# A decoder block on one core: the gate of the GLA branch applied in the merge instead of in the chunk loop

## The chip, the core and the metric

The kernel runs on one core of one Trainium2 chip. A core has five engines with a queue of instructions each, which they take in order: TensorE (PE; its weight loads are listed apart as PEld), VectorE (DVE), ScalarE (ACT), GpSimd (POOL) and SyncE (SP). Here SP does nothing but issue the DMA transfers. The engines wait for each other by semaphores. The metric is the device time of one execution in microseconds, and the median of several runs stands for a kernel.

## The reference

One layer of a hybrid decoder block on 1024 tokens with 1024 channels, all in float32: a Mamba-2 branch (SSD) and a gated linear attention (GLA) side by side, a merge of the two, cross-attention to 256 memory tokens and a SwiGLU FFN. What the change touches is the end of the GLA branch and the merge:

```
def gla_mixer(q, k, v, r, a1, w_a2, b_a, norm_g):
    ...                                     # chunked scan: o of shape (token, head, 256)
    o = rmsnorm(o, norm_g).reshape(Bsz, S, GLA_DV)
    return (o * jax.nn.silu(r.astype(jnp.float32))).astype(q.dtype)

def hybrid_mixer(n, ...):
    ...
    merged = jax.nn.sigmoid(g_ssd) * (y_ssd @ w_up_ssd) + jax.nn.sigmoid(g_gla) * (y_gla @ w_up_gla)
    return merged @ w_o

h = h + hybrid_mixer(rmsnorm(h, norm_mix), ...)
```

The norm works on each head's 256 channels, so its weights are a vector of 256, and two columns of 128 serve all eight blocks of 128 channels. The gate r, the two gates g and the queries, keys and values all come out of one large product with `w_in`.

## The kernel before

Activations lie with channels on the partitions: eight blocks of 128 channels by 1024 tokens, or 512 tokens for a half. Every float32 operand of a large product is split into a high and a low part in TensorE's faster float32 format (`split`, line 223: a copy on ACT, a subtraction on DVE), and three products are added up. The products with `w_in` and with the FFN's weights are done by a Strassen-Winograd scheme of seven products (`Unit`), the merge's products directly (`dense`, line 1192).

The program is written as Python generators that `run` (line 439) interleaves: for each step of the main one, so many steps of the side ones as their rate says. What is written that way is a first order only. Each instruction has a priority by its place in the program, `ahead` and `prio` put some before others, and a planner orders each engine's instructions from modelled times. That order is then fixed: on the chip an engine whose next instruction is not ready stands still, even if a later one could go.

Stages that matter here, by their time in the profiled execution:

- SSD, to about 660 us. Beside it, products for r, q, k and the first gates run on TensorE; r goes ungated to `sr_d` in DRAM.
- GLA, about 660 to 832 us (`GLA`, line 999, and `gla_steps`, line 1082). Eight chunks of 128 tokens run beside the products for the gates `gs` and `gg`, with a priority 1000 places ahead. For each chunk `load` and `load_qk` fetch queries, keys, decays, r and values by SP. `decay` multiplies queries and keys by exponentials (Exp on ACT, the products on DVE). `attend` makes the scores and transposes the keys (their copy is `kt`). `out` computes the chunk's output, and its Squares with accumulation (line 1065), a root on DVE and POOL, and a scaled copy (line 1068) make the norm. `scan` updates the state. `norm` transposes the output on PE; DVE takes it out of PSUM, multiplies by the norm's weights and by Silu(r), and writes it into the buffer of the queries and keys, which is stored to `yg_d`. `gate` is the Silu, one ACT instruction of 128x1024. It stands at the end of a chunk for the next one, while r is loaded two chunks ahead. `qk`, `sr`, `bd` and `v` have two buffers each.
- The merge, from 846 us. Three products in a row, each eight output blocks by two halves of tokens, 24 matmuls of 512 columns apiece: `y_ssd @ w_up_ssd`, `y_gla @ w_up_gla`, and the merged one with `w_o`. Beside the first, `fetch` (line 1214) loads `yg_d` by blocks of channels into the operand buffers of the second, and splits them. The weights are split one output block ahead into a ring of two (`Left`, line 1146, the tile `wd`). After each output half `post_ys` or `post_yg` applies a Sigmoid on ACT and a multiplication on DVE (`gated`, line 1283). Half rows of other operands come through `quad` (line 1138), with six buffers, `ga`. `presum` (line 1236) prepares sums of the FFN's weights beside the three products: 55 steps, five for each 256 rows (a load of 1 MB, four sums and four stores of 256 KB).
- After that cross-attention, the FFN (1376 to 1980 us) and the last norm, which the change leaves as they are, but for the residual's sum (`residual`, line 1297).

```
        def load(s):
            ...
            s.sr = gl.tile([P, 8, CH], F32, name="sr", tag="sr", bufs=2)
            SP.dma_start(s.sr, sr_d[:, tk].rearrange("(k p) s -> p k s", p=P))
```

Of the kernel before, what the change touches and what calls it, by code (L numbers as in the profile page):

```python
# [9 lines left out]
F32 = mybir.dt.float32  # L10
F32R = mybir.dt.float32r
I32 = mybir.dt.int32
AF = mybir.ActivationFunctionType
ALU = mybir.AluOpType
AX = mybir.AxisListType

P = 128
TOK = 1024
D = 1024
NB = D // P  # L20
# [8 lines left out]
CH = 128  # L29
# [49 lines left out]
def block_kernel(ctx: ExitStack, tc: tile.TileContext, t: dict, out: bass.AP):  # L79
    nc = tc.nc  # L80
    now = [0.0]
    PE, ACT, SP = Tensor(nc.tensor, now), nc.scalar, nc.sync
    DVE, POOL = Meter(nc.vector, now, 0.06, 1.04e-3), Meter(nc.gpsimd, now, 0.08, 2.25e-3)
# [15 lines left out]
    def dram(name, *shape):  # L99
        return dr.tile(list(shape), F32, name=name, tag=name)  # L100

    xT_d = dram("xT_d", D, TOK)
    h1_d = dram("h1_d", D, TOK)
# [6 lines left out]
    sr_d = dram("sr_d", D, TOK)  # L110
    v_d = dram("v_d", TOK, D)
    gs_d = dram("gs_d", D, TOK)
    gg_d = dram("gg_d", D, TOK)
    ys_d = dram("ys_d", D, TOK)
    yg_d = dram("yg_d", D, TOK)
# [9 lines left out]
    def bank(dt=F32):  # L125
        return ps.tile([P, 512], dt, name="bank", tag="bank", bufs=4)

    add = lambda e, o, a, b: e.tensor_tensor(o, a, b, ALU.add)
    sub = lambda e, o, a, b: e.tensor_tensor(o, a, b, ALU.subtract)
    mul = lambda e, o, a, b: e.tensor_tensor(o, a, b, ALU.mult)  # L130
    ahead = lambda: tc.high_priority(offset=AHEAD)
    ALL = slice(0, HALF)
    half = lambda j: slice(j * HALF, (j + 1) * HALF)
# [60 lines left out]
    def col(name, i=0):  # L194
        which, at = gcol[name]
        return cols[:, which, at + i:at + i + 1]
# [26 lines left out]
    def split(src, hi, lo, e=None):  # L223
        ACT.activation(hi, src, AF.Copy)  # L224
        sub(e or DVE, lo, src, hi)
# [213 lines left out]
    def run(main, *rest, prio=0):  # L439

        owed = [0.0] * len(rest)
        for _ in main:
            for i, (g, rate) in enumerate(rest):
                owed[i] += rate
                while owed[i] >= 1.0:
                    owed[i] -= 1.0
                    with tc.high_priority(offset=prio):
                        next(g, None)
# [90 lines left out]
    for k in range(NB):  # L539
        p = bank()  # L540
# [298 lines left out]
    qk = w_in_units(Q0, 2, store_rows(q_d)) + w_in_units(K0, 2, store_rows(k_d))  # L839
# [25 lines left out]
    class SSD:  # L865
# [62 lines left out]
        def gate(s):  # L928
            s.y = sp_.tile([P, 4, CH], F32, name="y", tag="y", bufs=3)
            for k in range(4):  # L930
                DVE.scalar_tensor_tensor(s.y[:, k], s.L[:, k], dcol[:, s.g * 4 + k:s.g * 4 + k + 1],
                                         s.py[:, k * P:(k + 1) * P], ALU.mult, ALU.add)
            mul(POOL, s.y, s.y, s.L[:, 4:8])
            sq = sp_.tile([P, 4, CH], F32, name="sq", tag="sq", bufs=1)
            ACT.activation(sq, s.y, AF.Square)
            s.rd = sp_.tile([P, CH], F32, name="rd", tag="rd", bufs=2)
            DVE.tensor_reduce(s.rd, sq.rearrange("p k s -> p s k"), AX.X, ALU.add)
# [53 lines left out]
    gl = pool("gla", 1, stack=st4)  # L991
# [7 lines left out]
    class GLA:  # L999
# [3 lines left out]
            s.c, s.tk = c, slice(c * CH, (c + 1) * CH)  # L1003

        def load_qk(s):
            s.qk = gl.tile([P, 8, CH], F32, name="qk", tag="qk", bufs=2)
            for i, d in enumerate((q_d, k_d)):
                SP.dma_start(s.qk[:, 4 * i:4 * i + 4], d[:, s.tk].rearrange("(k p) s -> p k s", p=P))

        def load(s):  # L1010
            tk = s.tk
            s.bd = gl.tile([P, 4, CH], F32, name="bd", tag="bd", bufs=2)
            SP.dma_start(s.bd, bd_d[:, tk].rearrange("(k p) s -> p k s", p=P))
            s.sr = gl.tile([P, 8, CH], F32, name="sr", tag="sr", bufs=2)
            SP.dma_start(s.sr, sr_d[:, tk].rearrange("(k p) s -> p k s", p=P))
            s.v = gl.tile([P, D], F32, name="v", tag="v", bufs=2)
            SP.dma_start(s.v, v_d[tk, :])

        def gate(s):
            ACT.activation(s.sr, s.sr, AF.Silu)  # L1020

        def decay(s):
            e = gl.tile([P, 4, CH], F32, name="e", tag="e", bufs=1)
# [46 lines left out]
        def norm(s):  # L1070
            for a in range(2):
                p = bank()
                for b in range(4):
                    k = 2 * b + a
                    PE.transpose(p[:, b * P:(b + 1) * P], s.o[:, k // 2, (k % 2) * P:(k % 2) * P + P], ident)

                y, g = (x.rearrange("p (b a) s -> p a b s", a=2)[:, a] for x in (s.qk, s.sr))
                DVE.scalar_tensor_tensor(y, p.rearrange("p (b s) -> p b s", s=CH), col("gla_norm", a), g,
                                         ALU.mult, ALU.mult)
            SP.dma_start(yg_d[:, s.tk].rearrange("(k p) s -> p k s", p=P), s.qk)  # L1080

    def gla_steps():
        it = [GLA(c) for c in range(NCH)]
        it[0].load_qk()
        it[0].load()
        it[1].load_qk()
        it[1].load()
        yield
        it[0].decay()
        it[0].start()  # L1090
        yield
        it[0].attend()
        it[0].gate()
        yield
        for i, a in enumerate(it):
            b = it[i + 1] if i + 1 < len(it) else None
            c = it[i + 2] if i + 2 < len(it) else None
            a.out()
            yield
            if b and i:  # L1100
                b.load_qk()
            a.scan()
            yield
            if b:
                b.decay()
                b.start()
            yield
            a.norm()
            yield
            if b:  # L1110
                b.attend()
            if b:
                b.gate()
            if c:
                c.load()
            yield
# [11 lines left out]
    ysg_d = dram("ysg_d", D, TOK)  # L1128
# [9 lines left out]
    def quad(src, base, i, j):  # L1138
        q = rp.tile([P, HALF], F32, name="ga", tag="ga")
        SP.dma_start(q, src[base + i * P:base + (i + 1) * P, half(j)])  # L1140
        return q
# [41 lines left out]
    def hl(slots_, k):  # L1183
        if callable(slots_[k]):
            slots_[k] = slots_[k]()
        return slots_[k]
# [5 lines left out]
    def dense(no, ins, post, pre=lambda o, j: None, js=JS):  # L1192

        todo = [(o, j) for o in range(NB) for j in (js if o + 1 < NB else js[::-1])]
        got = [pre(*x) for x in todo[:2]]
        for n, (o, j) in enumerate(todo):
            w = left[NB * no + o]
            if n + 2 < len(todo):
                got.append(pre(*todo[n + 2]))
            cur = got[n]  # L1200
            p = acc()
            m = 0
            for k in range(NB):
                for a, b in ((0, 0), (0, 1), (1, 0)):
                    PE.matmul(p, w[:, a, k], ins[k][:, b, half(j)], start=m == 0, stop=m == 3 * NB - 1)
                    m += 1
            with ahead():
                post(o, j, p, cur)
            yield

    EVEN, ODD = ("op",) * 8, ("op",) * 6 + ("aux",) * 2
    i_ys, i_yg, i_wo, i_xq, i_q, i_xo = (paired(x) for x in (EVEN, ODD, EVEN, ODD, EVEN, EVEN))

    def fetch(src, dst):

        for k in range(NB):
            x = hl(dst, k)
            raw = x[:, 1].bitcast(F32)
            SP.dma_start(raw, src[k * P:(k + 1) * P, :])
            ACT.activation(x[:, 0], raw, AF.Copy)  # L1220
            sub(DVE, x[:, 1], raw, x[:, 0])
            yield

    get_ys = fetch(ys_d, i_ys)
    for n, _ in enumerate(group(gg[3:], B)):
        if n == 0:
# [7 lines left out]
    s1 = Stats(rp)  # L1234
# [25 lines left out]
    def quad_of(src):  # L1260
        return lambda o, j: quad(src, o * P, 0, j)
# [19 lines left out]
        return got_g[n][j]  # L1281

    def gated(g, p):
        ACT.activation(g, g, AF.Sigmoid)
        mul(DVE, g, p, g)

    def post_ys(o, j, p, g):
        gated(g, p)
# [5 lines left out]
        add(either(g), g, g, y)  # L1294
        into(i_wo, o, j, g)

    def residual(store, stats, gain, put):
        def post(o, j, p, q):
            add(DVE, q, p, q)
            SP.dma_start(store[o * P:(o + 1) * P, half(j)], q)  # L1300
            put(o, j, q, col(gain, o))
            stats.take(j, q)
        return post
# [7 lines left out]
    def waiting(g, n):  # L1311
        for _ in range(n):
            yield
        for _ in g:
            yield

    early = presum()
    run(dense(0, i_ys, post_ys, lambda o, j: gate(gs_d, o, j)), (fetch(yg_d, i_yg), 0.5), (waiting(early, 5), 1.0))
    run(dense(1, i_yg, post_yg, lambda o, j: (gate(gg_d, o, j), quad(ysg_d, o * P, 0, j))), (early, 1.0))
    run(dense(2, i_wo, residual(h1_d, s1, "norm_xattn", put_xq), quad_of(xT_d)), (early, 1.0))  # L1320


    kv = []
# [84 lines left out]
    for n in range(len(at) + 2):  # L1408
        a = at[n] if n < len(at) else None
        b = at[n - 1] if 0 < n <= len(at) else None  # L1410
# [17 lines left out]
    for u in range(D_FF // 256):  # L1428
# [5 lines left out]
        gate = Unit(t["w_ffn_in"], 0, 256 * u, post=gpost, key="aux")  # L1434
# [174 lines left out]
    for u in range(1, len(gu)):  # L1609
        gate, up = gu[u]  # L1610
# [8 lines left out]
    for x, (n, k, kn) in enumerate(todo):  # L1619
        name = CHAIN[n]  # L1620
# [58 lines left out]
```

## Time and profile before

| | us |
|---|---|
| median of three runs | 1998.22 |
| lowest and highest run | 1995.6, 1999.11 |
| profiled execution (first to last instruction) | 2000.0 |
| PE busy | 1933.5 |
| DVE busy | 1330.8 |
| ACT busy | 866.3 |
| POOL busy | 658.0 |
| GLA stage | 665 to 832 |
| first product of the merge | 846.4 to 933.4 |

The page gives no other time of the profiled execution than its span, which lies 1.8 us above the median. "Busy" is the time in which an engine has an instruction under way; matmuls are pipelined, so PE can be busy without being at its peak. An idle time of PE is put down to what released it. A line number can be that of a helper: line 73 is every DVE and POOL instruction, line 51 every matmul, line 55 every transpose. There the tile names tell which is meant: `whi` and `wlo` are a weight's split parts, `o` on a DVE row is an output of a `w_in` product, `o` on a row of lines 1065 and 1068 the GLA output.

### The profile page before, as it was taken

The page shows a single profiled execution, that of the slowest core. Times are in us where ns is not written, and L with a number is a line of the kernel's source. Part 1 is how long each engine was busy: PE and PEld are TensorE (multiplying, and loading weights), DVE is VectorE, ACT ScalarE, POOL GpSimd, SP SyncE. Part 2 cuts the span into 40 slices and gives each one's busy share as a digit, 9 for nine tenths or more (in the row PEclk, how much of TensorE's full clock was granted, in tenths as well). Part 3 has the DMA queues.
Part 4 walks back from the last instruction along what each step waited for, and adds up shares of the span by engine and source line. Part 5 has one row for each costly group of instructions (what it writes and reads, how often), then busy time and mean ns, then how long its engine had stood idle before and what let it go on. Part 6 is the DMA issues. An engine that isn't in the chain of part 4 may idle for free.

```text
span 2000.0 us, 26313 instructions
## 1 busy us (share of the span) xinstructions
PE 1933.5 (97%) x9772; PEld 1619.0 (81%) x9772; DVE 1330.8 (67%) x1869; ACT 866.3 (43%) x1486; POOL 658.0 (33%) x482
## 2 busy tenths in 40 slices
PE   6899999999999999999999999999999999999998
PEld 6799677787777877888888888877888888878887
DVE  5856579979887566643553427478777777784465
ACT  7434745455553555543223226453333333354243
POOL 3521253445654121112442100155444444430002
PEclk9899999999999999999999999999999999999999
DMA  9332233365663754697674310333224223176463
GB/s 303 137 123 76 97 127 116 107 199 162 181 192 103 213 162 158 226 394 242 252 249 163 106 43 22 126 124 124 79 90 134 93 85 119 72 269 220 153 228 126
DMA packets 242019, 309.59 MB, mean 155 GB/s; under 512 B 16586, under 2 KB 164276, under 8 KB 241892
## 3 DMA queue, kind: packets, MB, share of 16 engines
q1 hardware_dynamic: 241892, 307.92, 46.1%
q8 instruction: 77, 1.26, 0.3%
q14 instruction: 50, 0.41, 0.1%
HBM read 211.07 MB, written 96.80 MB: 154 GB/s over the span
## 4 chain that ended last, share of the span: by engine, by line
PE 69%; DVE 12%; DMA 7%; ACT 5%; issue 3%; POOL 3%; SPq 0%; POOLq 0%; DVEq 0%; ACTq 0%
PE acc L51 61%; PE bank L51 7%; DVE wlo L73 3%; DVE cv L73 2%; DVE o L73 1%; PE bank L55 1%; DMA raw<-in_w_in_dram 1%; DMA h_d<-ga 1%; DMA sr<-sr_d 1%; ACT whi L224 1%; DMA csb<-cs_d 1%; POOL sa L73 1%; DMA xt<-in_x_dram 1%; DMA fr<-act_d 1%; DVE fs L73 1%
## 5 line engine op out<-in xcount | busy, mean ns | idle before, releaser
L51 PE MATMUL acc<-hl,wd 128*128 128x512 f32 x1920 | 439.2, 390 | 0.2 <-DVE hl L73 0.2
L51 PEld LDWEIGHTS acc<-hl,wd 128*128 128x128 f32 x1920 | 360.0, 188 | 75.3 <-DVE hl L73 0.6
L73 DVE TENSOR_TENSOR wlo<-raw,whi 128x512 fp32r<-128x512 f32 x264 | 243.1, 925 | 64.9 <-ACT whi L224 64.5
L224 ACT ACTIVATE whi<-raw 128x512 fp32r<-128x512 f32 x272 | 169.7, 628 | 237.0 <-PE acc L51 208.1
L73 DVE TENSOR_TENSOR o<-acc,o 128x512 f32<-128x512 f32 (+1 forms) x256 | 172.5, 675 | 105.8 <-PE acc L51 91.1
L51 PE MATMUL acc<-fs 128*128 128x512 f32 (+1 forms) x792 | 156.0, 356 | 1.8 <-ACT o L1574 1.7
L51 PEld LDWEIGHTS acc<-fs 128*128 128x128 f32 x792 | 130.6, 189 | 22.8 <-ACT o L1574 2.1
L73 POOL TENSOR_TENSOR raw<-raw,sa 128x512 f32<-128x512 f32 x48 | 65.0, 1354 | 253.8 <-DVE wlo L73 250.8
L224 ACT ACTIVATE fs<-fr 128x1024 fp32r<-128x1024 f32 (+1 forms) x84 | 80.1, 984 | 112.9 <-PE acc L51 38.6
L73 DVE TENSOR_TENSOR fs<-fr,fs 128x1024 fp32r<-128x1024 f32 (+1 forms) x84 | 99.8, 1218 | 38.5 <-ACT fs L224 38.0
L224 ACT ACTIVATE whi<-sa 128x512 fp32r<-128x512 f32 x96 | 59.9, 627 | 107.5 <-PE acc L51 107.4
L73 POOL TENSOR_TENSOR sa<-raw 128x512 f32<-128x512 f32 x47 | 75.8, 1613 | 82.0 <-DMA raw<-in_w_in_dram 44.8
L73 DVE TENSOR_TENSOR wlo<-sa,whi 128x512 fp32r<-128x512 f32 x96 | 82.8, 863 | 19.0 <-ACT whi L224 17.6
L224 ACT ACTIVATE wd<-raw 128x1024 fp32r<-128x1024 f32 x40 | 42.2, 1058 | 104.9 <-PE acc L51 104.4
L73 DVE TENSOR_TENSOR wd<-raw,wd 128x1024 fp32r<-128x1024 f32 x40 | 53.9, 1349 | 50.5 <-ACT wd L224 50.0
L73 POOL TENSOR_TENSOR raw<-raw 128x512 f32<-128x512 f32 x48 | 83.0, 1730 | 5.0 <-DVE sa L73 5.0
L51 PE MATMUL acc<-B21h,whi 128*128 128x512 f32 x192 | 76.3, 398 | 3.1 <-ACT o L353 3.1
L51 PE MATMUL acc<-T1h,whi 128*128 128x512 f32 x192 | 76.3, 397 | 2.8 <-ACT whi L224 2.8
L51 PE MATMUL acc<-B22h,wlo 128*128 128x512 f32 x192 | 77.0, 401 | 1.2 <-DVE wlo L73 1.2
L51 PE MATMUL acc<-B22h,whi 128*128 128x512 f32 x192 | 75.2, 392 | 2.6 <-DVE o L73 1.5
L51 PE MATMUL acc<-T4h,whi 128*128 128x512 f32 x192 | 75.9, 395 | 1.5 <-DVE o L73 1.5
L51 PE MATMUL acc<-T1h,wlo 128*128 128x512 f32 x192 | 76.8, 400 | 0.5 <-DVE wlo L73 0.5
(386 smaller groups left out, 4771.6 us busy)
## 6 DMA issues: line engine op xcount, KB each, us to landing
raw<-in_w_in_dram SPq DMA_DIRECT2D x26, 1024.0 KB, 6.1
raw<-in_w_ffn_in_dram SPq DMA_DIRECT2D x22, 1024.0 KB, 6.3
act_d<-o SPq DMA_DIRECT2D x77, 256.0 KB, 2.1
fr<-act_d SPq DMA_DIRECT2D x35, 512.0 KB, 6.4
pre<-in_w_ffn_out_dram SPq DMA_DIRECT2D x11, 1024.0 KB, 6.1
fr<-down_d SPq DMA_DIRECT2D x20, 512.0 KB, 3.7
down_d<-pre SPq DMA_DIRECT2D x33, 256.0 KB, 5.2
raw<-in_w_xkv_dram SPq DMA_DIRECT2D x8, 1024.0 KB
```

The lines of the kernel that those rows point to most:

```text
L51: return s.e.matmul(o, x, y, **kw)
L55: return s.e.transpose(o, x, i)
L73: return f(*a, **kw)
L224: ACT.activation(hi, src, AF.Copy)
```

## The change

Five edits go together.

- `gate` and the load of `sr` leave the GLA loop. `norm` copies the transposed output from PSUM to the buffer with ACT, without weights or gate, so `yg_d` holds the normalized output alone.
- `qk` has three buffers, and `load_qk` fetches for the chunk after next, at the same place in the loop.
- In the merge `fetch_gated` stands in place of `fetch` for `yg_d`. It has sixteen steps of half a block, at rate 1.0 instead of eight at 0.5: the half row of r through `quad`, Silu on ACT, one DVE instruction that multiplies by the norm's weights and the gate, then the split.
- `gated` uses Tanh of half the argument. Since sigmoid(g) = (tanh(g/2) + 1) / 2, DVE multiplies by tanh + 1 in one instruction, and the result is twice the merged value. The residual after `w_o` takes it with a scale of 0.5, the other residual with 1.0, in one DVE instruction of two operations.
- `presum` starts twelve steps into the first product instead of five, and goes at rate 1.1 beside the second and the third.

```
         def load_qk(s):
-            s.qk = gl.tile([P, 8, CH], F32, name="qk", tag="qk", bufs=2)
+            s.qk = gl.tile([P, 8, CH], F32, name="qk", tag="qk", bufs=3)
...
         def load(s):
-            s.sr = gl.tile([P, 8, CH], F32, name="sr", tag="sr", bufs=2)
-            SP.dma_start(s.sr, sr_d[:, tk].rearrange("(k p) s -> p k s", p=P))
...
-        def gate(s):
-            ACT.activation(s.sr, s.sr, AF.Silu)
...
-                y, g = (x.rearrange("p (b a) s -> p a b s", a=2)[:, a] for x in (s.qk, s.sr))
-                DVE.scalar_tensor_tensor(y, p.rearrange("p (b s) -> p b s", s=CH), col("gla_norm", a), g,
-                                         ALU.mult, ALU.mult)
+                ACT.activation(s.qk.rearrange("p (b a) s -> p a b s", a=2)[:, a], p.rearrange("p (b s) -> p b s", s=CH),
+                               AF.Copy)
...
-            if b and i:
-                b.load_qk()
+            if c:
+                c.load_qk()
...
-            if b:
-                b.gate()
...
+    def fetch_gated(src, gate_src, dst):
+        for k in range(NB):
+            x = hl(dst, k)
+            raw = x[:, 1].bitcast(F32)
+            SP.dma_start(raw, src[k * P:(k + 1) * P, :])
+            for j in range(2):
+                g = quad(gate_src, k * P, 0, j)
+                ACT.activation(g, g, AF.Silu)
+                DVE.scalar_tensor_tensor(g, raw[:, half(j)], col("gla_norm", k % 2), g, ALU.mult, ALU.mult)
+                split(g, x[:, 0, half(j)], x[:, 1, half(j)])
+                yield
...
     def gated(g, p):
-        ACT.activation(g, g, AF.Sigmoid)
-        mul(DVE, g, p, g)
+        ACT.activation(g, g, AF.Tanh, scale=0.5)
+        DVE.scalar_tensor_tensor(g, g, 1.0, p, ALU.add, ALU.mult)
...
-    def residual(store, stats, gain, put):
+    def residual(store, stats, gain, put, scale=1.0):
         def post(o, j, p, q):
-            add(DVE, q, p, q)
+            DVE.scalar_tensor_tensor(q, p, scale, q, ALU.mult, ALU.add)
...
-    run(dense(0, i_ys, post_ys, lambda o, j: gate(gs_d, o, j)), (fetch(yg_d, i_yg), 0.5), (waiting(early, 5), 1.0))
-    run(dense(1, i_yg, post_yg, lambda o, j: (gate(gg_d, o, j), quad(ysg_d, o * P, 0, j))), (early, 1.0))
-    run(dense(2, i_wo, residual(h1_d, s1, "norm_xattn", put_xq), quad_of(xT_d)), (early, 1.0))
+    run(dense(0, i_ys, post_ys, lambda o, j: gate(gs_d, o, j)), (fetch_gated(yg_d, sr_d, i_yg), 1.0), (waiting(early, 12), 1.0))
+    run(dense(1, i_yg, post_yg, lambda o, j: (gate(gg_d, o, j), quad(ysg_d, o * P, 0, j))), (early, 1.1))
+    run(dense(2, i_wo, residual(h1_d, s1, "norm_xattn", put_xq, 0.5), quad_of(xT_d)), (early, 1.1))
```

More of the change, by code (lines that the diff above doesn't have):

```diff
@@ L1092, in gla_steps @@
         it[0].attend()
-        it[0].gate()
         yield
```

## The prediction

> **What bounds the kernel now.** I read the busy times of the page first, then the windows by stage, then who waited for whom in the GLA stage, then the single instructions around one idle time of the tensor engine.
>
> ```profile
> span 2000.0 us, 26313 instructions
> PE 1933.5 (97%) x9772; PEld 1619.0 (81%) x9772; DVE 1330.8 (67%) x1869; ACT 866.3 (43%) x1486; POOL 658.0 (33%) x482
> ```
>
> PE is busy for all but 66.5 us. The change leaves every matmul as it is, so it can win time only where PE idles or its clock drops, and lose time only by making new idle. The windows tell where. Their columns are: stretch, its length, then busy time and count of PE, PEld, DVE, ACT and POOL, granted clock, DMA share, GB/s.
>
> ```profile
> 665.00:832.00 167.00, 159.35 (x771) 132.86 (x769) 98.95 (x194) 90.83 (x188) 36.45 (x29) 0.99 0.56 172
> 730.00:735.00 5.00, 5.00 (x24) 4.71 (x25) 5.00 (x10) 1.99 (x4) 3.22 (x3) 0.66 0.24 84
> 846.40:933.40 87.00, 87.00 (x385) 72.05 (x384) 37.14 (x37) 33.87 (x45) 16.55 (x12) 1.00 0.90 326
> 880.00:890.00 10.00, 10.00 (x46) 8.29 (x45) 3.05 (x3) 1.13 (x3) 0.00 (x0) 1.00 1.06 397
> ```
>
> The first row is the GLA stage: PE idles for 167 - 159.35 = 7.65 us. The second is the stretch after its longest idle time, at a granted clock of 0.66: 5 x 0.34 = 1.7 us lost. The third is the first matrix product of the merge, where the new work lands: PE has no idle time there, DVE and ACT are about 40% busy. In the fourth, inside the third, the DMA engines are full at 397 GB/s. The waits of the GLA stage (total us, times, longest):
>
> ```profile
> DVE qk L73 <- DMA qk<-q_d: 37.3, 6, 6.7
> ACT L1020 <- DMA sr<-sr_d: 30.1, 6, 7.3
> PE bank L55 <- ACT o L1068: 5.8, 4, 2.1
> PE acc L51 <- DVE o L73: 1.5, 1, 1.5
> ```
>
> 5.8 + 1.5 us are nearly all of PE's 7.65. One idle time of each kind, by its instructions (start, duration, and in brackets the idle time before it and what ended it):
>
> ```profile
> 713.58 2.12 SPq L1015 DMA_DIRECT2D sr<-sr_d  x1
> 719.20 0.59 PE L51 MATMUL bank<-sm,qk 128*128 128x256 f32 x2
> 720.19 1.28 ACT L1020 ACT_TABLE_LOAD   x1 [6.60 <-DMA sr<-sr_d]
> 721.49 1.06 ACT L1020 ACTIVATE sr<-sr 128x1024 f32<-128x1024 f32 x1
> 723.08 1.28 ACT L1024 ACT_TABLE_LOAD   x1
> 724.92 0.36 ACT L1065 ACTIVATE o<-bank 128x256 f32<-128x256 f32 x1
> 726.77 0.22 ACT L1065 ACTIVATION_READ_ACCUMULATOR o<-bank 128x1 f32 x1
> 728.83 0.33 PE L55 MATMUL bank<-ident,o 128*128 128x128 f32 x1 [2.06 <-ACT o L1068]
> ...
> 701.09 0.87 DVE L73 SCALAR_TENSOR_TENSOR qk<-qk,e 128x512 f32<-128x512 f32 x1 [6.74 <-DMA qk<-q_d]
> 707.90 0.47 PE L51 MATMUL acc<-B22h,whi 128*128 128x512 f32 x1 [1.53 <-DVE o L73]
> ```
>
> ACT takes its instructions in order. It stands 6.60 us before the Silu of a later chunk's r, because that load was issued only at 713.58: it has to wait until the buffer is freed by the norm of the chunk two before. The chunk's output products end near 719.8 and their Squares could follow, but they start at 724.92, behind Silu and two table loads; so PE comes to the transposes of `o` at 726.77 and waits 2.06 us. In the other case DVE stands 6.74 us before the queries, and PE then waits 1.53 us for a sum that is queued behind. Both loads are the ones that the change touches. The last chunk has neither in front of it:
>
> ```profile
> 823.70 0.59 PE L51 MATMUL bank<-sm,qk 128*128 128x256 f32 x2
> 824.96 0.20 ACT L1065 ACTIVATION_READ_ACCUMULATOR o<-bank 128x1 f32 x1
> 826.49 1.57 ACT L1068 ACTIVATE o<-bank,ss 128x256 f32<-128x256 f32 x4 [1.32 <-POOL ss L73]
> 831.20 1.04 PE L55 MATMUL bank<-ident,o 128*128 128x128 f32 x8
> ```
>
> From the end of the products (824.29) to the scaled `o` (828.06) it takes 3.8 us, and PE's order has 6.9 us of other matmuls in between: 3.1 us to spare.
>
> **The change part by part.** *Silu(r) leaves GLA*, with eight loads of 512 KB on SP's queue. Off ACT go:
>
> ```profile
> L1020 ACT ACT_TABLE_LOAD x8 | 10.3, 1283 | 30.1 <-DMA sr<-sr_d 30.1
> L1024 ACT ACT_TABLE_LOAD x7 | 9.0, 1283 | 2.4 <-DMA bd<-bd_d 2.3
> L1020 ACT ACTIVATE sr<-sr 128x1024 f32<-128x1024 f32 x8 | 8.5, 1058 | 0.1
> L1035 ACT ACTIVATE kt<-bank 128x512 f32<-128x512 f32 x8 | 4.8, 596 | 7.6 <-PE bank L55 7.6
> ```
>
> 10.3 + 9.0 + 8.5 = 27.8 us of work (one load for Exp stays, so 26.5) and 30.1 us of waiting, some 7 us a chunk. The Squares at 724.92 would come at about 720, so `o` is ready at about 724, before PE gets there at 726.77. All four waits on L1068 go: 5.8 us. The longest of them is also the one in front of the slow clock: 1.7 us. What is late next is the chain Square, root, scaling itself, with the 3 us to spare of the last chunk.
>
> *The eviction after the transposes moves from DVE to ACT.* DVE loses 16 instructions:
>
> ```profile
> L73 DVE SCALAR_TENSOR_TENSOR qk<-bank,cols,sr x16: 734/742/751, 689.6 to 832.7; 128x512 f32<-128x512 f32 x16
> ```
>
> that is 11.9 us. ACT gains 16 copies out of PSUM at 596 ns (the `kt` row above): 9.5 us, 1.2 us a chunk, which wait for PE's transposes and have the copy of `kt` and a weight split queued behind them. In the chunk above that split could afford 1.03 us, in a later one only 0.79:
>
> ```profile
> 712.97 0.63 ACT L224 ACTIVATE whi<-sa 128x512 fp32r<-128x512 f32 x1 [1.03 <-PE acc L51]
> 796.65 0.64 ACT L224 ACTIVATE whi<-raw 128x512 fp32r<-128x512 f32 x1 [0.79 <-PE acc L51]
> ```
>
> Bounds: 0 (the split waits for a ring buffer anyway) and 8 x 1.2 = 9.5 us (every copy delays PE). I take 1.1 us, near the lower end: 1.2 - 1.03 and 1.2 - 0.79 are 0.2 to 0.4 us a chunk, some of it still covered by the ring.
>
> *Queries and keys two chunks ahead.* The third buffer costs 4 KB a partition against 8 KB freed by `sr`. The load for chunk a+2 is issued where that for a+1 was, and still behind the store of chunk a-1, since three buffers back is the same chunk as before. So SP's own wait stays, with the stores of gates and weight loads behind it:
>
> ```profile
> SPq L1008 <- DMA yg_d<-qk: 10.4, 6, 2.5
> ```
>
> but the data are needed a chunk, some 21 us, later. DVE's 37.3 us of waiting goes, and with it PE's 1.5 us.
>
> *The merge's fetch.* In place of eight copies and eight subtractions of 128x1024, sixteen steps of a half: load of 256 KB, Silu, product, copy, subtraction.
>
> ```profile
> L1220 ACT ACTIVATE hl<-hl 128x1024 fp32r<-128x1024 f32 x12 | 12.6, 1056 | 6.8 <-DMA hl<-yg_d 6.4 <-DMA hl<-ys_d 0.4
> L224 ACT ACTIVATE wd<-raw 128x1024 fp32r<-128x1024 f32 x8 | 8.5, 1062 | 32.5 <-PE acc L51 32.5
> L1284 ACT ACTIVATE gates<-gates 128x512 f32<-128x512 f32 x12 | 6.8, 619 | 6.8 <-DMA gates<-gg_d 6.2 <-DMA gates<-gs_d 0.6
> L73 DVE TENSOR_TENSOR hl<-hl 128x1024 fp32r<-128x1024 f32 x12 | 15.1, 1296 | 1.3 <-ACT hl L1220 1.3
> L73 DVE TENSOR_TENSOR gates<-acc,gates 128x512 f32<-128x512 f32 x8 | 5.5, 691 | 20.8 <-PE acc L51 20.8
> ```
>
> ACT: 32 x 0.62 - 8 x 1.06 = 11.4 us more, 33.9 to 45.3 of 87.0. DVE: 16 x (0.74 + 0.69) - 8 x 1.30 = 12.5 us more, 37.1 to 49.6. The cover is the spare time of both beside a saturated PE. What PE needs from them is one pair of split weights per output block of 87.0 / 8 = 10.9 us, and ACT now waits 32.5 / 8 = 4.1 us for PE before each. DMA: 4.2 MB more, and seven steps of the weight sums for the FFN, five steps to 2 MB, are put off past this stage: 2.9 MB less. So 326 becomes (326 x 87 + 1300) / 87 = 341 GB/s, under the 397 of the full stretch. The new loads go through SP and the six `ga` buffers, so a load waits for the step six before it; POOL gets nothing of it. Cost: 0; if the cover fails, the price is the second rival's.
>
> *Tanh for Sigmoid, and the doubled result halved in the residual.* Equally many ACT instructions; on DVE a two-operation instruction replaces multiplications of 691 ns and the residual's sums, 0.05 us more each (742 against 691) for 64 instructions, or nothing: under 3.2 us of hidden DVE time. The later weight sums (rates 1.1) run beside the next two products: 0.
>
> The sum: 2000.0 - 5.8 - 1.5 - 0.3 (rest of the 7.65) - 1.7 + 1.1 = 1991.8 us for the profiled execution. That one is 1.8 us above the median of the runs shown (1998.22), so 1990.0 us. A measurement of this kernel tells a change of about 0.2%, 4 us.
>
> **The rivals.** *The compiled order eats the gain.* The instruction order is planned from modelled times; with less work in front of the Squares the transposes may be put earlier, and PE waits on Square, root and scaling. For it: the whole order is planned anew. Against it: between products and transposes stand 7.0 us of other matmuls where Silu was in between (719.8 to 726.77) and 6.9 us in the last chunk, where it was not, so the planned gap does not hang on Silu. If 0.7 us stays in each of eight chunks, 5.6 us come back: 1995.6.
>
> *Slower: the wait moves to the merge.* Two steps fall in each 10.9 us block, and ACT has 45.3 / 8 = 5.7 us of work in it. If each Silu stands in front of its load, ACT becomes the bound as soon as a wait exceeds (10.9 - 5.7) / 2 = 2.6 us. With the 5.0 us that a Silu waited in GLA (30.1 / 6) a block takes 15.7 us and eight lose 38 us: 2028. At 3.2 us a wait the 9 us gained are gone. For it: the DMA engines are full there. Against it: the fetch in the same stretch waited 6.4 us in all, and these loads have no buffer to wait for but the ring of six.
>
> *Tables.* The trace shows Silu and Exp loading tables against each other in every chunk, and Sigmoid loading one at 853.71, with no Exp between it and the last Silu at 804.61. Whether Tanh and Silu need one each no row shows. If all 16 Tanh and 16 Silu alternate, 32 loads of 1.283 us put ACT at 45.3 + 41.1 = 86.4 of 87.0 us; with the 12.6 us (6.4 + 6.2) that it already waits for DMA there, 12 us would show: 2002. If the two halves of a block run together it is half of that and hidden: 1990. I take one load, as this stage has now, since the order puts several of a kind together (four `gates` in a row at 890.83).
>
> ```profile
> 804.61 1.06 ACT L1020 ACTIVATE sr<-sr 128x1024 f32<-128x1024 f32 x1
> 853.71 1.28 ACT L1284 ACT_TABLE_LOAD   x1 [3.29 <-DMA whi<-gs_d]
> 890.83 2.27 ACT L1284 ACTIVATE gates<-gates 128x512 f32<-128x512 f32 x4
> ```
>
> [...]
>
> **How the numbers follow.** Forecast (1986 to 1994): 0.65. First rival (1994 to 2000): 0.16. Second (2000 to 2028): 0.10. Tables (1990 to 2002): 0.06. Something else, slower: 0.03. The forecast's own low end: all 9.3 us gone and no new wait gives 1988.9, less the 2.6 us by which the fastest run lies under the median, 1986. The high end is 2000, where forecast, first rival and half of the tables' cases are in. Faster by over 0.2% are the forecast and a part of the first rival and of the tables (0.04 + 0.03): 0.72; within 0.2%: 0.13; slower: 0.15.
>
> **What would show it.** Right: in the GLA stage no table load beside the first, no wait of DVE for `q_d`, ACT not waiting for `sr_d`, PE idle under 2 us, no slow clock; in the first product of the merge PE without idle time, ACT near 45 us, one table load. Wrong: waits of PE for L1068 as before (first rival), waits of PE for `wd` in the merge with ACT before them waiting for `sr_d` (second), many table loads after 840 us (third), or new waits for `whi` behind the copies in GLA.

## The result, and the profile after

| | before | after |
|---|---|---|
| median, us (20 runs each, measured together) | 1998.16 | 1994.05 |
| profiled execution, us | 2000.0 | 1990.4 |

The ratio is 0.9978, with a 95% interval of 0.9970 to 0.9987: the changed kernel is 4.1 us faster, about half of the 8.2 us forecast (1998.22 to 1990.0). The two profiled executions lie 9.6 us apart. Of that 4.7 us arise before the GLA stage, where the order of the instructions on PE, DVE and ACT is the same in both kernels. This is scatter between executions and no effect of the change; the stages from GLA on make up the other 4.9 us.

The page after, in the same two lines:

```profile
span 1990.4 us, 26352 instructions
PE 1930.4 (97%) x9772; PEld 1620.2 (81%) x9772; DVE 1331.3 (67%) x1878; ACT 859.4 (43%) x1503; POOL 659.0 (33%) x481
```

The windows after (stretch, length, busy time and count of PE, PEld, DVE, ACT, POOL, granted clock, DMA share, GB/s):

```profile
665.00:832.00 167.00, 167.00 (x825) 142.23 (x824) 100.07 (x190) 83.65 (x193) 37.49 (x28) 1.00 0.54 175
730.00:735.00 5.00, 5.00 (x23) 4.11 (x23) 5.00 (x15) 2.62 (x10) 1.34 (x1) 1.00 0.45 141
826.00:913.00 87.00, 87.00 (x385) 71.78 (x384) 51.33 (x63) 42.38 (x65) 11.42 (x8) 1.00 0.99 365
880.00:890.00 10.00, 10.00 (x46) 8.29 (x45) 10.00 (x10) 7.40 (x13) 6.35 (x4) 1.00 1.04 406
1020.00:1130.00 110.00, 104.11 (x458) 85.91 (x457) 42.59 (x50) 31.41 (x46) 31.30 (x23) 0.97 0.53 178
1050.00:1055.00 5.00, 1.58 (x4) 1.29 (x5) 5.00 (x5) 1.24 (x2) 3.67 (x3) 0.64 0.86 304
1055.00:1060.00 5.00, 5.00 (x17) 3.94 (x16) 4.09 (x6) 3.39 (x5) 2.19 (x2) 0.68 0.43 137
1060.00:1065.00 5.00, 5.00 (x24) 4.14 (x23) 2.47 (x3) 1.25 (x2) 1.91 (x2) 1.00 0.36 107
```

In the GLA stage PE has no idle time left (167.00 of 167.00, 159.35 before) and the clock stays at 1.00, also where it was 0.66. The merge's first product now begins 20 us earlier (826.4 us; 4.7 us of that are the scatter, and some 3 us come from twelve matmuls that stood ahead of it and now stand behind its first eight) and keeps PE busy all the time, with the DMA engines as full as before (406 GB/s). The loss is in the fifth row, the merge's third product: 5.89 us idle, and two stretches, at its end and behind it, at a clock of 0.64 and 0.68. Before, that place had next to none:

```profile
1020.00:1130.00 110.00, 109.78 (x491) 90.47 (x490) 48.09 (x55) 34.29 (x50) 34.84 (x24) 1.00 0.56 190
```

The waits of the GLA stage after (total us, times, longest):

```profile
DVE qk L73 <- DMA qk<-q_d: 16.4, 5, 5.5
PEld bank L55 <- ACT o L1063: 0.2, 1, 0.2
```

PE's four waits for the scaled `o` are gone (the scaling is line 1063 now). One chunk by its instructions, as it was shown of before:

```profile
709.96 0.59 PE L51 MATMUL bank<-sm,qk 128*128 128x256 f32 x2
711.21 0.37 ACT L1060 ACTIVATE o<-bank 128x256 f32<-128x256 f32 x1
714.60 1.57 ACT L1063 ACTIVATE o<-bank,ss 128x256 f32<-128x256 f32 x4 [1.32 <-POOL ss L73]
717.38 0.27 PE L55 MATMUL bank<-ident,o 128*128 128x128 f32 x1
```

The products end at 710.55 and the Squares start 0.66 us later; before, it was 5.1 us (719.8 to 724.92). The scaled `o` is ready at 716.17, and PE comes to the transposes at 717.38 without a wait.

The new stall, by its instructions:

```profile
1041.66 0.38 SPq L1245 DMA_DIRECT2D pre<-in_w_ffn_out_dram  x1
1046.78 1.27 POOL L73 TENSOR_TENSOR sa<-pre 128x512 f32<-128x512 f32 x1 [7.39 <-DMA pre<-in_w_ffn_out_dram]
1048.13 1.26 POOL L73 TENSOR_TENSOR pre<-sa,pre 128x512 f32<-128x512 f32 x1
1049.43 1.73 DVE L73 TENSOR_TENSOR pre<-pre 128x512 f32<-128x512 f32 x1 [9.49 <-POOL pre L73]
1051.09 0.68 DVE L73 SCALAR_TENSOR_TENSOR ga<-acc,ga 128x512 f32<-128x512 f32 x1
1051.69 1.68 DVE L73 TENSOR_TENSOR wd<-raw,wd 128x1024 fp32r<-128x1024 f32 x1
1053.42 11.84 PE L51 MATMUL acc<-hl,wd 128*128 128x512 f32 x41 [5.89 <-DVE wd L73]
```

The last row is one group of matmuls; its 11.84 us are the group's length. Row by row: the load of the last MB of FFN weights for `presum` is issued at 1041.66, and POOL begins the first sum at 1046.78. The fourth sum of that round stands on DVE and needs the result of POOL's second, so DVE stands still for 9.49 us in front of it. Behind it in DVE's order are a residual's sum and the low part of the next weight block, `wd`, for which PE then waits. In before all 44 sums of `presum` are on POOL; here it is 43, and the 44th is this one. Which engine a sum goes to is chosen while the order is planned (`either`: POOL unless DVE is free more than 1.0 us sooner by modelled times).

### The profile page after: what moved, and what is told of

It is laid out like the page before. It is cut to its first block, busy times and chain, and to the rows that moved or that the text cites. A ratio compares the mean times of both kernels' runs of the same rounds, so it can differ in the third digit from the quotient of the medians.

```text
span 1990.4 us, 26352 instructions
## 1 busy us (share of the span) xinstructions
PE 1930.4 (97%) x9772; PEld 1620.2 (81%) x9772; DVE 1331.3 (67%) x1878; ACT 859.4 (43%) x1503; POOL 659.0 (33%) x481
## 5 line engine op out<-in xcount | busy, mean ns | idle before, releaser
L51 PE MATMUL acc<-B21h,wlo 128*128 128x512 f32 x192 | 75.9, 396 | 0.9 <-DVE wlo L73 0.9
```

The lines of the kernel that those rows point to most:

```text
L51: return s.e.matmul(o, x, y, **kw)
```

## Experiments

The theory after reading the traces: (A) the missing half went into that one sum on DVE. Its rivals: (B) the later and faster `presum` (start after 12 steps, rate 1.1) loads the DMA or POOL too late as such; (C) one of the other edits gives time back in a way that these windows don't show. For the gain itself: (E) ACT's wait for r made PE wait, against (F) the work of Silu and its table switches did. In the expectations e1 is the first run below and e3 the one with queries and keys alone.

Besides medians I use one number worked out from each trace: each matmul's start less the start of the one before, less the median of that step for its shape, summed over a stretch. It contains idle time, slow clock and small stretchings. It is 27.2 us for before and 14.8 for after between 700 and 900 us, and 0.3 and 8.3 between 1000 and 1100: 12.4 us gained and 8.0 given back, 4.4 net, beside 4.1 by the medians. Only its differences mean something between 700 and 900 us: 14.6 us of it remain in kernels whose PE is never idle in the GLA stage. Below it is "GLA excess" and "third-product excess".

**All sums on POOL.**

```
         def presum():
-            e = lambda: either(s1_, 1.0)
+            e = lambda: POOL
```

> The changed kernel with one edit: the sums of the FFN weights beside the merge (presum) are all given to POOL, none to DVE. Theory A: the gain of the GLA stage was partly given back in the third product of the merge by one subtraction that the planner's choice put on DVE, where it stood 9.5 us in front of a weight split; with it on POOL the 5.9 us wait of PE for wd and the 6.8 us at half clock behind it (3.4 us lost) go, and the time is about 9 us under the changed kernel, 13 us under the one before: near 1985. Rival B: the wait belongs to the late load and the store ring of that stage, whichever engine does the subtraction, and PE waits somewhere else for as long: no change against the changed kernel, near 1994.

Measured: 1987.81 us against 1999.65 for before on the same chip, ratio 0.9940 (0.9927 to 0.9953). The window of the third product:

```profile
1020.00:1130.00 110.00, 109.89 (x493) 90.93 (x492) 44.72 (x51) 32.58 (x48) 32.34 (x25) 1.00 0.56 187
```

PE has no stall there, the third-product excess is -0.2 and the GLA excess 14.6. In the order of the instructions nothing else differs from the changed kernel: one sum is gone from DVE and stands on POOL. So the gain becomes 11.8 us instead of 4.1: the one sum on DVE cost 7.7 us, by the two intervals some 3 us more or less. The GLA stage gained 12.6 us (27.2 less 14.6), which leaves next to nothing for C.

**The old timing of `presum`.**

```
-    run(dense(0, ...), (fetch_gated(yg_d, sr_d, i_yg), 1.0), (waiting(early, 12), 1.0))
+    run(dense(0, ...), (fetch_gated(yg_d, sr_d, i_yg), 1.0), (waiting(early, 5), 1.0))
...
-    run(dense(1, ...), (early, 1.1))
-    run(dense(2, ...), (early, 1.1))
+    run(dense(1, ...), (early, 1.0))
+    run(dense(2, ...), (early, 1.0))
```

> The changed kernel with the old timing of presum (start after 5 steps, rate 1.0 beside each of the three products); the choice between POOL and DVE stays free, and here it falls on POOL for all 44 sums. Theory A (it is the engine, not the timing): as in e1, near 1985. Rival C (the sums pushed later collide with the third product): faster than e1, or e1 not faster and this one near 1985.

Measured: 1987.75 us, 0.9943 (0.9930 to 0.9956), the same as with POOL alone. With this timing all 44 sums go to POOL, though nobody says so. PE gets one wait of 1.5 us for `wd` in the first product. The late pace itself costs nothing measurable, since the run before keeps it and is as fast; what it did was to move one choice of the planner. B, which the expectation calls rival C, falls.

**The same sum put on DVE in the kernel before.**

```
-            sub(e(), a(0, 1), a(0, 1), a(1, 1))
+            sub(DVE if k == KP - 1 else e(), a(0, 1), a(0, 1), a(1, 1))
```

> The kernel before with one edit: the fourth sum of the last of the eleven rounds of presum goes to DVE, as the planner had it in the changed kernel; everything of the change is left out. Theory A: that one instruction, which waits for POOL's sum and a load, stands in front of weight splits on DVE and PE waits for wd: 3 to 9 us over before, near 2005. Rival: without the later start of presum DVE waits for nothing there, and the time is that of before within 2 us.

Measured: 2008.82 against 1997.81 us, 1.0054 (1.0036 to 1.0072), 11 us slower. Its windows, and PE's waits of the merge:

```profile
1020.00:1130.00 110.00, 103.55 (x448) 85.20 (x447) 43.67 (x52) 33.34 (x49) 30.03 (x21) 0.97 0.55 180
1045.00:1050.00 5.00, 1.69 (x4) 1.40 (x5) 4.52 (x6) 1.69 (x3) 0.32 (x1) 0.61 0.97 361
```

```profile
PE acc L51 <- DVE wd L73: 6.4, 1, 6.4
```

The same wait and the same slow clock come with nothing of the change in the kernel, whose orders differ from those of before by this one sum alone. A is shown from both sides. The third-product excess is 8.8 us, so 2 to 3 us of the 11 are not located, and the 11 us lie above the 3 to 9 expected.

**Queries and keys two chunks ahead, alone on before.** A vector of the cross-attention is moved to another pool (`mbc` from `ep` to `vp`) to make room for the third buffer.

```
-            s.qk = gl.tile([P, 8, CH], F32, name="qk", tag="qk", bufs=2)
+            s.qk = gl.tile([P, 8, CH], F32, name="qk", tag="qk", bufs=3)
...
-            if b and i:
-                b.load_qk()
+            if c:
+                c.load_qk()
```

> The kernel before with only the queries and keys two chunks ahead in three buffers (a small unrelated tile moved to another pool to make room); Silu, its loads and the tables stay in GLA. Theory: PE's 1.5 us wait behind the queries goes, the four waits for the scaled output (5.8 us) and the slow clock (1.7 us) stay: 1 to 2 us under before, near 1996.5. Rival D: the late queries are what holds the chunk up, and the Silu's wait only covers it: 6 us or more under before.

Measured: 1995.36 us against 1999.65, 0.9979 (0.9969 to 0.9989), 4.3 us, between the 1 to 2 us of the theory and the 6 us of rival D. The GLA window and all that PE waits for in it:

```profile
665.00:832.00 167.00, 162.02 (x790) 135.10 (x789) 103.88 (x200) 89.15 (x189) 36.34 (x28) 1.00 0.59 183
```

```profile
PE bank L55 <- ACT o L1068: 4.7, 4, 1.6
```

The wait for `DVE o` is gone, and so is the slow clock, which the theory had left in place; the longest of the other waits is now 1.6 us and not 2.1. GLA excess 22.6.

**The sums on POOL, queries and keys one chunk ahead again.** The edit of the first run, and the one above undone in it.

> As e1, but queries and keys in two buffers, loaded one chunk ahead as before. Theory: with Silu out of the way PE keeps at most the one wait behind the queries, 1.5 us of idle time in GLA: 1 to 2 us over e1, near 1986.5. Rival D: the waits for the scaled output come back, since the exponentials' products on DVE still stand before the late queries: 6 us or more over e1.

Measured: 1985.77 us, 0.9933 (0.9921 to 0.9945); PE is busy for all of the GLA stage, GLA excess 14.6. Queries two chunks ahead win time only while Silu is in the loop; with Silu out they are worth nothing, not even the 1 to 2 us expected. This is the fastest kernel of the study by its median, though its interval overlaps that of the first run.

**The sums on POOL, Sigmoid in place of Tanh.**

```
-        ACT.activation(g, g, AF.Tanh, scale=0.5)
-        DVE.scalar_tensor_tensor(g, g, 1.0, p, ALU.add, ALU.mult)
+        ACT.activation(g, g, AF.Sigmoid)
+        mul(DVE, g, p, g)
```

(and the residual's scale 1.0.)

> As e1, but with Sigmoid and a multiplication in the merge instead of Tanh, so that Sigmoid and Silu alternate there. The planned order has ten table loads in the merge instead of one: 9 x 1.283 = 11.5 us more on ACT. Theory: the first product keeps PE busy without a gap, since ACT has some 40 us to spare in it; same time as e1 within 2 us, near 1987.8. Rival (tables): the loads stand in front of weight splits and PE waits for wd: 5 to 12 us over e1.

Measured: 1987.40 against 1997.81 us, 0.9944 (0.9927 to 0.9961), the same as with Tanh. The table loads of the merge between 820 and 940 us, first after, then this run (count, busy us, ns of one):

```profile
L1223 ACT ACT_TABLE_LOAD x1 | 1.3, 1283 | 0.0
```

```profile
L1223 ACT ACT_TABLE_LOAD x5 | 6.4, 1283 | 0.1
L1288 ACT ACT_TABLE_LOAD x5 | 6.4, 1283 | 0.1
826.00:913.00 87.00, 87.00 (x385) 71.84 (x384) 51.55 (x63) 54.63 (x75) 12.20 (x8) 1.00 0.99 366
```

Tanh and Silu took one load together here, Sigmoid and Silu, in this order, ten. ACT is busy for 54.6 of 87 us with them, and PE does not notice.

**The sums on POOL, the transposed output taken out by DVE in place of ACT.**

```
-                ACT.activation(s.qk.rearrange(...)[:, a], p.rearrange(...), AF.Copy)
+                DVE.tensor_copy(s.qk.rearrange(...)[:, a], p.rearrange(...))
```

> As e1, but the transposed output of GLA is copied out of PSUM by DVE instead of ACT, 16 copies. Theory: no wait of PE hangs on which of the two does it, now that Silu is gone; same time as e1 within 2 us. Rival: the 1.2 us a chunk on ACT delays the weight splits (the prediction's term of 1.1 us), and this one is 1 to 9 us faster.

Measured: 1990.47 us, 0.9957 (0.9941 to 0.9974), which overlaps the run with ACT's copies. PE is busy all through GLA again. In the merge's first product PE has two small waits for DVE, 0.8 us for `gates` and 0.4 us for `wd`. ACT's copies cost PE nothing in GLA, and by these times it can't be told which of the two engines makes them faster. The planner laid the instructions out anew for this kernel.

**Before with three buffers for r.**

```
-            s.sr = gl.tile([P, 8, CH], F32, name="sr", tag="sr", bufs=2)
+            s.sr = gl.tile([P, 8, CH], F32, name="sr", tag="sr", bufs=3)
```

> The kernel before with three buffers for r in GLA instead of two (the same small tile moved as in e3), so that its load need not wait for the norm of the chunk two before; Silu, its table loads and everything else stay where they are. Theory E: it is the 30.1 us of waiting for r that holds the Squares up, not the 27.8 us of Silu and table loads: PE's waits behind the scaled output go, PE's idle time in GLA falls from 7.65 to under 3 us, and the time is 5 to 8 us under before, near 1992.5. Rival F: Silu and the tables alone are enough: PE's idle time stays over 5 us, and the time within 3 us of before.

Measured: 1998.02 against 1997.81 us, 0.9999 (0.9987 to 1.0010): no change. The waits stayed, and SP's queue tells why:

```profile
ACT L1020 <- DMA sr<-sr_d: 25.6, 5, 5.6
PE bank L55 <- ACT o L1068: 7.0, 6, 1.9
...
729.20 0.37 SPq L1080 DMA_DIRECT2D yg_d<-qk  x1
729.62 0.57 SPq L1015 DMA_DIRECT2D sr<-sr_d  x1
```

The load of r stands in SP's queue right behind the store of a chunk's output, and that store waits for DVE's norm. Another buffer doesn't bring the load forward. So this run decides nothing between E and F, but it refutes that the buffer alone held the load. It has no slow clock in GLA either (granted clock 1.00); its longest wait is 1.9 us.

**Before with r's load ahead of that store.** Three buffers as above, and the load issued at the head of the loop's step.

```
+        def load_sr(s):
+            s.sr = gl.tile([P, 8, CH], F32, name="sr", tag="sr", bufs=3)
+            SP.dma_start(s.sr, sr_d[:, s.tk].rearrange("(k p) s -> p k s", p=P))
...
         for i, a in enumerate(it):
...
+            if c:
+                c.load_sr()
             a.out()
```

> The kernel before with r in three buffers and its load issued one step of the loop earlier, ahead of the chunk's products and so ahead of the store of the chunk now being worked on in SP's queue (the same 0.56 KB made room for as in the run with three buffers alone). Silu, its table switches and the norm stay in the GLA. Theory E: ACT's wait for sr_d falls from 25 us to under 8, PE's waits behind the output's scaling go, its idle time between 665 and 832 us is under 2 us, and the time is 5 to 9 us shorter. Theory F: ACT's wait for sr_d falls as well, but PE's idle time stays at 5 us or more and the time within 2 us of before. The planner lays the instructions out anew, so a difference of 2 us alone decides nothing.

Measured: 1993.32 against 1997.39 us, 0.9980 (0.9971 to 0.9989), 4.1 us. The GLA window, ACT's wait (its line is 1022 here), and what is left of PE's waits but for 0.3 us:

```profile
665.00:832.00 167.00, 164.20 (x800) 138.61 (x799) 102.98 (x202) 93.57 (x192) 37.83 (x29) 0.99 0.61 187
```

```profile
ACT L1022 <- DMA sr<-sr_d: 14.3, 5, 4.6
PE acc L51 <- DVE o L73: 2.4, 2, 1.9
```

With all eight Silus and fourteen of fifteen table loads still there, PE no longer waits for the scaled `o`. That speaks for E, but not alone: ACT's wait is halved and not under 8 us, PE's idle time is 2.80 us and not under 2, and 4.1 us fall short of the 5 to 9 expected. Nor is it the load alone that changed, since the planner laid the instructions out anew. In before four chunks make PE wait; their Squares start 2.9 to 5.3 us after the end of the chunk's products, and PE comes to the transposes some 7 us after it. Here the Squares of the same chunks start at most 3.2 us after the products, and the transposes stand at 6.8 to 9.4 us. So the Squares are earlier, as E has it, and the transposes are later too.

**Before with Copy in place of Silu.**

```
-            ACT.activation(s.sr, s.sr, AF.Silu)
+            ACT.activation(s.sr, s.sr, AF.Copy)
```

> The kernel before with one word changed: the gate of the GLA runs Copy in place of Silu, so this kernel leaves Silu(r) of the GLA's output out of the computation. The order of the instructions on every engine is that of the kernel before, except that the fourteen switches of ACT's table inside the GLA fall away; the load of r, ACT's wait for it and an instruction of the same shape stay. Theory E (ACT stands in front of r's late load, and that is what makes PE wait): the wait of ACT for sr_d stays near 25 us in sum, PE's idle time between 665 and 832 us stays at 5 to 7.6 us, the time within 2 us of before. Theory F (it is the work of Silu and the table switches, 14 x 1.28 us, that makes the norms late): PE's idle time there falls under 2 us and the time is 5 to 8 us shorter.

Measured: 1994.82 us, 0.9984 (0.9973 to 0.9995), 2.6 us. The GLA window and waits:

```profile
665.00:832.00 167.00, 161.26 (x781) 134.78 (x780) 102.57 (x199) 72.73 (x175) 37.59 (x28) 0.99 0.57 179
```

```profile
ACT sr L1020 <- DMA sr<-sr_d: 31.4, 7, 7.4
PE bank L55 <- ACT o L1068: 4.6, 3, 2.1
```

The orders on PE, DVE and POOL are those of before. Without the table switches ACT has 18 us less to do and still stands before r as long as before (31.4 us), and PE still waits 4.6 of 5.8 us; it is idle for 5.74 us, as E expected, and the time is a little further under before than the 2 us that E allowed. So F's forecast of under 2 us of idle time fails, and the switches are worth less than the earlier load: GLA excess 24.7, 2.5 us under before, against 22.4 with the earlier load, 4.8 under. Neither alone gives the 12.4 of the change, which takes both off and the other loads of r from the queue too. How the rest divides between these is open.

## Why the prediction was right in sign and half in size

*PE's four waits on the scaling, 5.8 us, and the slow stretch, 1.7 us.* Right: both are gone after. Of the mechanism, that the work of the table switches alone is not enough is shown by the run with Copy (4.6 of 5.8 us stay); that the late load was the main thing is supported by the run with the earlier load, whose order on PE differs too. The whole of the 7.65 us of idle time went. The gain in GLA was larger than forecast: 12.4 us by starts against 9.3, the other 3 us being, by this count, small stretchings that the summed idle times don't contain.

*"it has to wait until the buffer is freed by the norm of the chunk two before".* Incomplete, as three buffers for r without any effect showed. The load stands behind the store of the same chunk in SP's queue, and the store waits for the same norm. The forecast's number did not hang on which of the two it was.

*ACT's copies after the transposes, 1.1 us.* Too much: 0. PE never waits for a split behind them in after, and the run with DVE's copies is not faster.

*Queries and keys two chunks ahead, 1.5 us.* The idle time went, but the credit was given to the wrong edit. Alone on before they give 4.3 us, on top of Silu's removal nothing. And "no wait of DVE for `q_d`" was named as a sign of being right: 16.4 us of 37.3 are left. The rows of the decays show why. SP issues a load, and DVE's next decay starts as soon as it lands:

```profile
688.59 0.36 SPq L1008 DMA_DIRECT2D qk<-q_d  x1
692.94 0.85 DVE L73 SCALAR_TENSOR_TENSOR qk<-qk,e 128x512 f32<-128x512 f32 x1 [3.29 <-DMA qk<-q_d]
...
762.43 0.69 DVE L73 SCALAR_TENSOR_TENSOR qk<-qk,e 128x512 f32<-128x512 f32 x1 [1.91 <-DMA qk<-q_d]
```

With the load a chunk earlier the planner put the decay earlier as well, the last one at 762.43, 50 us ahead of the last store (812.50); in before it is 27 us (807.26 to 833.98). DVE stands in front of the load again, but PE, which is never idle in this stage, waits for nothing behind it.

*The merge's fetch, 0.* Right. ACT is busy for 42.4 us of the first product (45.3 forecast), DVE for 51.3 (49.6), the DMA engines move 365 GB/s (341), and PE has no idle time. Silu waits 0.2 us in all for `sr_d`, so the second rival's mechanism did not appear there.

```profile
L1223 ACT ACTIVATE ga<-ga 128x512 f32<-128x512 f32 x16 | 9.5, 620 | 0.4 <-DMA ga<-sr_d 0.2
```

*Tanh, 0.* Right, and one table load, as assumed. The ten loads of the run with Sigmoid cost nothing, so the third rival would have needed more than that; its 32 were not tried. The mixed order of Sigmoid and Silu took ten loads of 1283 ns against one, but with ACT at 54.6 of 87 us no reload reached PE.

*"The later weight sums (rates 1.1) run beside the next two products: 0."* This is the step that failed. The term measured 7.7 us (4.1 against 11.8 us, the change with and without the sum on DVE). The trace has 8.3 us in that place: 5.9 of PE's wait, and 2.4 of slow matmuls behind it. Of these the windows show 17 between 1055 and 1060 where the next 5 us at full clock have 24, 5 x (1 - 17/24) = 1.5 us, and the rest lies in the 1.58 us ahead. The prediction looked at the sums' place and not at their engine; it named the compiled order as a rival, but only for the transposes in GLA. The sign that it gave for the second rival, waits of PE for `wd` in the merge, did appear, but in the third product and with DVE in front, not ACT. With this term at 0, as the two runs without the sum on DVE have it, the change gives 11.8 us, and the forecast of 8.2 would have been too low rather than too high. The range of 1986 to 2000 held the time with either. That it did is partly the width of the range and partly luck: the gain in GLA was forecast 3 us too small, which made up for some of the 8 us that were not foreseen.

## What to carry to other kernels

An edit that only shifts side work in time can move an automatic choice of engine, and one instruction that waits for late data, put on the engine that prepares the next weights, cost here two thirds of what five edits had won (7.7 of 11.8 us); so compare, after such an edit, which engine each side instruction got. A load can be late for its queue as well as for its buffer (here three buffers for r left the time at 0.9999 of before): read which instruction stands before it in the issuing queue before adding a buffer. Where two edits take away the same wait, the second can be worth nothing, whatever it is worth alone: here 4.3 us alone, and nothing behind the other.

## What the runs showed of the hardware that was not expected

- Two idle times of PE of nearly the same length were followed by different clocks. With r's load early, PE idled 1.91 us up to 709.16, and the granted clock between 710 and 715 us was 0.66; in before it idled 1.95 us up to 792.26, and the clock from 790 to 800 us was 1.00. What makes the difference was not shown, and no run was made to test it. The run with r's load early, then before:

```profile
709.16 0.47 PE L51 MATMUL acc<-B22h,whi 128*128 128x512 f32 x1 [1.91 <-DVE o L73]
705.00:710.00 5.00, 3.02 (x13) 1.88 (x12) 5.00 (x12) 1.78 (x8) 2.65 (x2) 1.00 0.45 157
710.00:715.00 5.00, 5.00 (x24) 4.47 (x25) 3.88 (x8) 2.65 (x7) 0.00 (x0) 0.66 0.28 105
```

```profile
792.26 1.64 PE L55 MATMUL bank<-ident,o 128*128 128x128 f32 x8 [1.95 <-ACT o L1068]
790.00:795.00 5.00, 3.02 (x23) 2.19 (x21) 3.85 (x11) 3.00 (x9) 1.02 (x1) 1.00 0.14 52
795.00:800.00 5.00, 5.00 (x25) 4.16 (x23) 3.68 (x7) 2.34 (x4) 1.28 (x1) 1.00 0.53 157
```

- The third product has little to spare. In the profiled execution of the run with Copy for Silu, whose PE, DVE and POOL have the same order as before, PE waited 2.9 us there (clock 0.97), nearly all of it at 1092.43 for ACT's part of the next weight block. ACT had stood 15.26 us in front of a load for the cross-attention, `kT_d`, that SP issued only at 1087.93:

```profile
1020.00:1130.00 110.00, 107.13 (x468) 87.91 (x466) 45.87 (x51) 32.66 (x48) 33.62 (x24) 0.97 0.53 172
1087.93 0.37 SPq L1328 DMA_DIRECT2D ga<-kT_d  x1
1090.80 0.63 ACT L224 ACTIVATE kvhl<-ga 128x512 fp32r<-128x512 f32 x1 [15.26 <-DMA ga<-kT_d]
1092.43 1.22 PE L51 MATMUL acc<-hl,wd 128*128 128x512 f32 x2 [2.58 <-ACT wd L224]
```

  In before ACT stands 11.68 us in front of the same load, and PE doesn't wait. Why SP issued it late here, and how often this happens in unprofiled executions, is open.
